# A hybrid decoder layer on one core: state layout, order of the value projections and of the SSM outputs in the mixing stage

## The chip, the core and the metric

The kernel runs on one core of a Trainium2 chip. The metric is the device time of one execution in microseconds. Three runs of the kernel before took 994.3, 994.25 and 993.5 us; the median is 994.25 us.

The engines are named as in the profile: PE (TensorE, matrix products, with PEld for its weight loads), DVE (VectorE), ACT (ScalarE), POOL (GpSimd) and SP (SyncE, whose queue issues nearly all DMAs here). Each engine works through its own queue in order and waits for others on semaphores.

## What is computed

One decoder layer for 512 tokens of width 1024, in float32: a SwiGLU block, a mixing stage and a second SwiGLU block, each between two RMS norms. The change lies in the mixing stage:

```python
h = rms_norm(x, mix_pre_g[l])
proj = h @ w_mix_in[l]                       # (512, 1024) @ (1024, 2048)
q, k, v, u = jnp.split(proj, [512, 1024, 1536], axis=-1)
attn = dilated_attention(q, k, v)            # 8 heads of 64, ALiBi, three dilations
ssm = s5_mixer(u, ...)                       # 32 groups of 16 channels, 64 complex states
mixed = jnp.concatenate([attn, ssm], axis=-1) @ w_mix_out[l]
x = x + rms_norm(mixed, mix_post_g[l])
```

The S5 mixer runs the recurrence state(t) = a * state(t-1) + B u(t) over the 512 tokens, reads out y = Re(C state) + D u, and returns gelu(y) * sigmoid(gelu(y) @ w_glu + b_glu).

## The kernel before

Activations lie transposed: channels on the 128 partitions, 512 tokens along the free axis. Every large product is split into three, with weights and activations as a high and a low part (`mm3`, L123: high x high, high x low, low x high). A weight tile arrives by one DMA as `wraw` (3 buffers), ACT casts the high part `whi` (L91), and DVE, or POOL where `pool=True`, subtracts to get the low part `wlo` (L93).

**The mixing stage** (`mix`, L821) has these pieces of PE work, in an order that the program fixes by hand:

- Projections (`proj`): 16 chunks of 128 output channels, 24 matmuls each. A generator `pieces` hands them out in halves of 12 matmuls; `f()` runs one half. Chunks 0 to 3 are q, 4 to 7 k, 8 to 11 v (two heads each), 12 to 15 u. DVE takes each result from PSUM as qT, kT or vT (L842, L844).
- Scores (`attn_scores`, L759) of a head pair `hp`: PE writes q*k, DVE adds the bias and takes the row extremum `nm` (L782), ACT takes the exponential and its row sum `den` (L784), DVE the reciprocal `rd` (L786), and the rows are scaled: those of the first head on ACT (L790), those of the second on DVE (L792).
- `turn` (L796) transposes the scaled scores on PE and copies them on ACT (L808); `turn_v` (L870) does it for v (copy `vn` on ACT, L876); `values` multiplies them into `pv`, which ACT and DVE split into the high and low parts of `cat`.
- The SSM: chunks of T = 4 tokens, 128 chunks in 8 super-chunks of 16. `states` (L881) computes each chunk's own contribution to the states `Hs`; `scan` (L1032), a generator whose steps are handed out by `go()`, or by `fg()` together with a projection half, runs on DVE alone: 15 steps inside all super-chunks at once, then 7 carry steps from super-chunk to super-chunk (`car`), then the carries multiplied back into all positions, 4 of 16 state blocks at a time. `outputs` (L888) computes four blocks of y from the shifted states and the weights `w2`, and the gelu.
- Output tiles (`out_attn`, `mo`, weights `wmoa`) for the attention half; `glu` with weights `wgl` for the gated SSM half (result `so`); the SSM half of the output product is done in `boundary` (L255, `yt`, weights `tw` loaded by `load_tail` from `wmot`), together with the norms and the first products of the next stage.

In `Hs` the chunk index is (super-chunk, position) with the position innermost, so that one scan step reads and writes every 16th element (64 bytes apart):

```python
h = Hs.rearrange("p q n (s i) -> p q n s i", i=SI)
step(h[:, :, :, :, i], h[:, :, :, :, i - 1], b1(pw[:, 0, :, 0]), b1(pw[:, 1, :, 0]), [NP, SC])
```

Instructions wrapped in `fix` keep the order of the program; the others are placed between them when the program is built. The order of the pieces of the stage is:

```python
sc = scores(1); f(); states(0); states(4); turn_v(0); states(8); states(12)
for hp in (2, 3):
    sc = scores(hp); fg(2); turn_v(hp - 1); fg(); values(hp - 1, pt)
```

## Time and profile before

| | |
|---|---|
| Median of three runs | 994.25 us |
| Profiled execution, its own time | 996.23 us |
| Span of its trace, first to last instruction | 994.4 us |
| Busy share of the span | PE 96%, DVE 55%, ACT 37%, POOL 23% |
| Mean granted TensorE clock | 0.981 of full speed |
| Chain that ended last | PE 84%, DVE 8%, issue 3%, ACT 3% |

A profile shows one execution. A row of its timeline gives start, duration, engine, line, operation and tile; in brackets the idle time before it and what ended the idle time. "Windows" are stretches of the span with each engine's busy time and the granted clock. The trace calls the tiles `w1` and `w2` both `w`. The mixing stage lies between about 404 and 589 us of the span, and the boundary to the second SwiGLU block behind it.

### The profile page before, as it was taken

Reading aid. Unit: us, or ns where it says so; the run is one execution under the profiler, and the core shown is the slowest. Engines: PE = TensorE matmul, PEld = TensorE weight load, DVE = VectorE, ACT = ScalarE, POOL = GpSimd, SP = SyncE. Lnnn points to the kernel's source line nnn. Section 1 sums busy time; section 2 is a strip of 40 time slices with the busy share of each in tenths; the row PEclk is TensorE's granted clock in tenths of the full one; section 3 lists DMA queues with packets and bytes.
Section 4 is the critical chain, followed back from the end, with each engine's and each line's share of the span. In section 5 each row is a group of like instructions: output and inputs, shape, how many; then the busy total and the mean of one; then the engine's idle time right before and its main releaser. Section 6 shows DMA issues by size and latency. Waiting matters only on the chain.

```text
span 994.4 us, 12883 instructions
## 1 busy us (share of the span) xinstructions
PE 958.3 (96%) x5088; PEld 800.3 (80%) x5088; DVE 544.7 (55%) x938; ACT 367.9 (37%) x604; POOL 231.8 (23%) x135
## 2 busy tenths in 40 slices
PE   9999999999999999999798789999999999999996
PEld 7888888888888899777566679888888888888885
DVE  7997124552356449467879656664215532554326
ACT  7353234521233225184443634444323222232312
POOL 2322122222233134200000423522013202321300
PEclk9999999999999999999899889999999999999998
DMA  7323334443333320661212620132332323233302
GB/s 256 105 86 111 116 102 148 131 148 103 106 127 106 106 86 22 191 191 59 64 33 96 202 64 23 52 97 85 106 107 85 102 92 103 85 106 126 107 1 85
DMA packets 38605, 102.48 MB, mean 103 GB/s; under 512 B 7664, under 2 KB 10736, under 8 KB 38000
## 3 DMA queue, kind: packets, MB, share of 16 engines
q1 hardware_dynamic: 37680, 98.50, 31.2%
q10 hardware_dynamic: 864, 3.15, 0.9%
q8 instruction: 40, 0.66, 0.3%
q14 instruction: 21, 0.17, 0.1%
HBM read 94.03 MB, written 7.60 MB: 102 GB/s over the span
## 4 chain that ended last, share of the span: by engine, by line
PE 84%; DVE 8%; issue 3%; ACT 3%; DMA 1%; POOL 1%; SPq 0%; DVEq 0%; POOLq 0%; ACTq 0%
PE gu L119 45%; PE yo L119 20%; PE yt L119 6%; PE prj L119 4%; PE first L119 4%; ACT sc L784 1%; DVE Hs L1035 1%; DVE xl L142 1%; PE pv L119 1%; DVE wlo L93 1%; PE st L119 1%; DVE x L301 1%; DVE sx L1035 1%; PE pt L806 1%; PE gl L119 1%
## 5 line engine op out<-in xcount | busy, mean ns | idle before, releaser
L91 ACT CAST whi<-wraw 128x1024 fp32r<-128x1024 f32 (+5 forms) x161 | 155.9, 970 | 323.9 <-PE gu L119 128.1
L93 POOL TENSOR_TENSOR wlo<-wraw,whi 128x1024 fp32r<-128x1024 f32 (+2 forms) x63 | 159.0, 2523 | 480.2 <-ACT whi L91 480.2
L119 PE MATMUL gu<-xh,whi 128*128 128x512 f32 x656 | 257.5, 393 | 0.0
L119 PE MATMUL gu<-xh,wlo 128*128 128x512 f32 x656 | 255.4, 389 | 0.0
L119 PE MATMUL gu<-xl,whi 128*128 128x512 f32 x656 | 255.3, 389 | 0.0
L93 DVE TENSOR_TENSOR wlo<-wraw,whi 128x1024 fp32r<-128x1024 f32 (+5 forms) x98 | 112.8, 1154 | 114.4 <-ACT whi L91 114.0
L119 PEld LDWEIGHTS gu<-xh,wlo 128*128 128x128 f32 x656 | 123.1, 188 | 26.0
L119 PEld LDWEIGHTS gu<-xh,whi 128*128 128x128 f32 x656 | 123.2, 188 | 25.0 <-issue 0.4
L119 PEld LDWEIGHTS gu<-xl,whi 128*128 128x128 f32 x656 | 123.2, 188 | 24.9
L394 DVE TENSOR_TENSOR ut<-gu,rs 128x512 f32<-128x512 f32 x41 | 28.3, 689 | 103.7 <-PE gu L119 103.7
L139 DVE TENSOR_TENSOR al<-ut,ah 128x512 fp32r<-128x512 f32 x44 | 69.0, 1569 | 25.0 <-ACT ah L138 24.8
L93 POOL TENSOR_TENSOR tw<-wraw,tw 128x1024 fp32r<-128x1024 f32 x8 | 19.4, 2430 | 163.7 <-ACT tw L91 163.7
L392 DVE TENSOR_TENSOR gt<-gu,rs 128x512 f32<-128x512 f32 x41 | 28.2, 689 | 50.8 <-PE gu L119 50.8
L119 PE MATMUL yo<-ah,whi 128*128 128x512 f32 x144 | 56.0, 389 | 0.0
L119 PE MATMUL yo<-al,whi 128*128 128x512 f32 x144 | 56.0, 389 | 0.0
L119 PE MATMUL yo<-ah,wlo 128*128 128x512 f32 x144 | 56.0, 389 | 0.0
L119 PE MATMUL yo<-whi,ah 128*128 128x512 f32 x144 | 56.0, 389 | 0.0
L119 PE MATMUL yo<-wlo,ah 128*128 128x512 f32 x144 | 56.0, 389 | 0.0
L119 PE MATMUL yo<-whi,al 128*128 128x512 f32 x144 | 56.0, 389 | 0.0
L138 ACT CAST ah<-ut 128x512 fp32r<-128x512 f32 x44 | 27.2, 621 | 58.2 <-DVE ut L395 58.2
L119 PE MATMUL first<-xl,whi 128*128 128x256 f32 (+1 forms) x144 | 44.5, 309 | 2.5 <-DVE xl L142 2.3
L119 PE MATMUL first<-xh,whi 128*128 128x256 f32 (+1 forms) x144 | 44.5, 309 | 0.9 <-ACT xh L141 0.9
(188 smaller groups left out, 1478.6 us busy)
## 6 DMA issues: line engine op xcount, KB each, us to landing
wraw<-w2i SPq DMA_DIRECT2D x44, 512.0 KB, 3.5
wraw<-w1i SPq DMA_DIRECT2D x42, 512.0 KB, 3.5
wraw<-w2o SPq DMA_DIRECT2D x18, 512.0 KB, 3.4
wraw<-wmi SPq DMA_DIRECT2D x16, 512.0 KB, 3.6
wraw<-w1o SPq DMA_DIRECT2D x16, 448.0 KB, 3.3
x<-xT SPq DMA_DIRECT2D x8, 256.0 KB, 4.5
w1d<-w1s SPq DMA_DIRECT2D x8, 256.0 KB, 2.8
w2d<-zb SPq DMA_DIRECT2D x2, 1024.0 KB, 4.9
```

Source lines behind the costliest of these rows:

```text
L91: fix(self.nc.scalar.copy(out=hi, in_=raw))
L93: fix(eng.tensor_tensor(out=lo, in0=raw, in1=hi.bitcast(F32), op=ALU.subtract))
L119: i = self.nc.tensor.matmul(*a, **k)
L138: nc.scalar.copy(out=hi, in_=src)
L139: nc.vector.tensor_tensor(out=lo, in0=src, in1=hi.bitcast(F32), op=ALU.subtract)
L142: fix(nc.vector.scalar_tensor_tensor(out=lo, in0=src, scalar=scale, in1=hi.bitcast(F32), op0=ALU.mult, op1=ALU.subtract))
L301: fix(nc.vector.tensor_tensor(out=xk, in0=t, in1=xk, op=ALU.add))
L392: nc.vector.tensor_tensor(out=gt, in0=o[f][0], in1=r, op=ALU.mult)
L394: nc.vector.tensor_tensor(out=ut, in0=o[f][1], in1=r, op=ALU.mult)
L784: nc.scalar.activation(out=so, in_=so, func=AF.Exp, bias=nm[:, t:t + 1], scale=-1.0, accum_out=den[:, t:t + 1])
L806: self.fix(nc.tensor.transpose(b[i][:, o:o + P], sc[:, c:c + P], self.ident))
L1035: tt = lambda o, x, y, op: self.fix(self.nc.vector.tensor_tensor(out=o, in0=x, in1=y, op=op))
```

## The change

The parts are these.

1. `states` writes the states with the position outermost and the super-chunk innermost (`(i s)`, `(s i)` before), one position later than before, and the last position into a tile of its own, `ends`. One scan step then touches runs of 8 neighbouring elements. The carries are kept in position 0 of `Hs` itself, with zero for the first super-chunk, so `outputs` reads 128 columns instead of 127 shifted ones. There are 6 carry steps instead of 7; the last part handles 15 positions x 8 super-chunks (480 elements an operation) instead of 7 x 16 (448). The reordering of u (`uT`) writes the new order; `glu`'s result is put back into the order of tokens where `so` is written.
2. A head pair's v projection comes ahead of its predecessor's scores: `f()` ahead of `scores(1)`, `fg(5)` for `fg(4)`, `fg()` for `fg(2)` behind `scores`, `fg(3)` for `fg(2)` at the end.
3. For head pairs 0 and 1 both heads are scaled on DVE; for 2 and 3 both on ACT, and the reciprocal is a power of -1 on POOL.
4. `outputs(0)` to `outputs(3)` stand between the output tiles 3 to 6; `w2` takes `wraw` buffers (before: `whi`). `glu` runs its first two tiles over three of four input blocks, then the fourth; both `wgl` tiles are loaded ahead; `zg` is scaled on ACT ahead of `glu`. `go(...)` counts follow.
5. The low halves of `tw` and `wgl` are made on DVE (POOL before).
6. `boundary` starts with tiles 0 and 1 over three of four input blocks, then the fourth for both.

```diff
+        b2 = [self.bank("yt")[:, :HT] for _ in range(2)]
+        for ks in (range(NT - 1), (NT - 1,)):
+            for m in range(2):
+                for k in ks:
+                    th, tl = tail(k)
+                    self.mm3(b2[m], tw[0][:, m, k], tw[1][:, m, k], th[:, hs[0]], tl[:, hs[0]], k == 0, k == NT - 1)
...
-            nc.vector.reciprocal(out=rd, in_=den)
+            if hp < 2:
+                nc.vector.reciprocal(out=rd, in_=den)
+            else:
+                nc.gpsimd.tensor_tensor(out=rd, in0=den, in1=self.mone, op=ALU.pow)
...
-                if i == 0:
+                if hp < 2:
+                    nc.vector.tensor_scalar_mul(so, so, rd[:, t:t + 1])
+                else:
                     nc.scalar.activation(out=so, in_=so, func=AF.Copy, scale=rd[:, t:t + 1])
-                else:
-                    nc.vector.tensor_scalar_mul(so, so, rd[:, t:t + 1])
...
-            dj = lambda v: v.rearrange("p (c j) -> p j c", j=T)
-            nc.vector.tensor_tensor(out=ut.rearrange("p (j c) -> p j c", j=T), in0=dj(o0[m]), in1=dj(r), op=ALU.mult)
+            nc.vector.tensor_tensor(out=ut.rearrange("p (j i s) -> p s i j", j=T, s=SC),
+                                    in0=o0[m].rearrange("p (s i j) -> p s i j", j=T, s=SC),
+                                    in1=r.rearrange("p (s i j) -> p s i j", j=T, s=SC), op=ALU.mult)
...
-                nc.scalar.copy(out=Hs[:, c, n4:n4 + 4].rearrange("p n k -> p (n k)"), in_=b)
+                b = b.rearrange("p (n k) -> p n k", k=NCH)
+                nc.scalar.copy(out=Hs[:, c, n4:n4 + 4, SC:], in_=b[:, :, :NCH - SC])
+                nc.scalar.copy(out=ends[:, c, n4:n4 + 4], in_=b[:, :, NCH - SC:])
...
-            w2 = self.wp.tile([P, 2, 4, P], F32, name="w2", tag="whi", bufs=4)
+            w2 = self.wp.tile([P, 2, 4, P], F32, name="w2", tag="wraw", bufs=3)
...
-        sc = scores(1)
         f()
+        sc = scores(1)
...
-        fg(4)
+        fg(5)
         for hp in (2, 3):
             sc = scores(hp)
-            fg(2)
+            fg()
...
-        tail = lambda c: self.load_tail(a["wmot"], c, True)
+        tail = lambda c: self.load_tail(a["wmot"], c, False)
...
         for n4 in range(4):
             outputs(n4)
+            if n4 < 3:
+                if n4 == 0:
+                    go()
+                out_attn(4 + n4)
+                tail(n4)
...
+        for m in range(2):
+            glu(m, range(3))
+        for m in range(2):
+            glu(m, (3,))
+        glu(2)
         tail(3)
+        glu(3)
         out_attn(7)
...
-        h = Hs.rearrange("p q n (s i) -> p q n s i", i=SI)
+        h = Hs.rearrange("p q n (i s) -> p q n i s", s=SC)
...
-            step(h[:, :, :, :, i], h[:, :, :, :, i - 1], b1(pw[:, 0, :, 0]), b1(pw[:, 1, :, 0]), [NP, SC])
+            step(ends if i == SI - 1 else h[:, :, :, i + 1], h[:, :, :, i], b1(pw[:, 0, :, 0]), b1(pw[:, 1, :, 0]),
+                 [NP, SC])
```

How this moves instructions is seen at three places. The first is DVE's queue at the scores of head pair 2 (`ISA sc,nm` is the bias and extremum, `vT` the value projection of head pair 1, `sx` and `Hs` the scan). Before, the end of that group of scores:

```order
L782 ISA sc,nm<-sc,bias 128x256
L782 ISA nm 128x1
L786 RECIPROCAL rd<-den 128x4 x2
L792 TENSOR_SCALAR sc<-sc,rd 128x128
L792 TENSOR_SCALAR sc<-sc,rd 128x256
L792 TENSOR_SCALAR sc<-sc,rd 128x384
L792 TENSOR_SCALAR sc<-sc,rd 128x512
L844 TENSOR_TENSOR vT<-prj,rs 128x512
```

Now, the beginning of that group:

```order
L1064 TENSOR_TENSOR Hs<-Hs,sx 128x16x8 x2
L858 TENSOR_TENSOR vT<-prj,rs 128x512
L1064 TENSOR_TENSOR sx<-pw,Hs 128x256 x2
L1064 TENSOR_TENSOR Hs<-Hs,sx 128x32x8
L793 ISA sc,nm<-sc,bias 128x512
L793 ISA nm 128x1
```

vT stood behind the reciprocals and four scalings, and stands now ahead of the first row of scores; reciprocals and scalings have left the queue here.

The second is ACT's queue at the same place (`den` is written by the exponentials, `vn` is the transposed v). Before:

```order
L790 ACTIVATE sc<-sc,rd 128x384
L790 ACTIVATE sc<-sc,rd 128x512
L784 ACTIVATE sc,den<-sc,nm 128x384
L784 ACTIVATE sc,den<-sc,nm 128x256
L91 CAST whi<-wraw 128x1024
L876 COPY vn<-vt 128x512
```

Now:

```order
L806 ACTIVATE sc<-sc,rd 128x384
L806 ACTIVATE sc<-sc,rd 128x512
L795 ACTIVATE sc,den<-sc,nm 128x384
L795 ACTIVATE sc,den<-sc,nm 128x256
L892 COPY vn<-vt 128x512
L806 ACTIVATE sc<-sc,rd 128x128
```

`vn` keeps its place behind all eight exponentials and four scalings; four more scalings follow it.

The third is SP's queue of DMAs at the SSM outputs (`w<-w2d` is the tile `w2` of one `outputs`). Before:

```order
L97 DMA wraw<-wmoa 128x512 x3
L891 DMA w_4696<-w2d 128x2x512
L891 DMA w_4754<-w2d 128x2x512
L97 DMA wraw<-wmot 128x1024
L891 DMA w_4812<-w2d 128x2x512
L97 DMA wraw<-wmoa 128x512
L891 DMA w_4870<-w2d 128x2x512
```

Now:

```order
L910 DMA w_4654<-w2d 128x2x512
L99 DMA wraw<-wmoa 128x512
L99 DMA wraw<-wmot 128x1024
L910 DMA w_4737<-w2d 128x2x512
L99 DMA wraw<-wmoa 128x512
L99 DMA wraw<-wmot 128x1024
L910 DMA w_4820<-w2d 128x2x512
L99 DMA wraw<-wmoa 128x512
L99 DMA wraw<-wmot 128x1024
L910 DMA w_4903<-w2d 128x2x512
```

Each `w2` now stands between the weights of two output tiles and shares their three buffers. By the waits of the built program the third `w2` is loaded into the buffer of the second and waits for PE's last read of it, the end of `outputs(1)`; the fourth waits for the low half of output tile 6; the `wgl` tile behind it for `outputs(2)`, and the last `wmot` for `outputs(3)`.

More of the change, by code (lines that the diff above doesn't have):

```diff
@@ L58, in __init__ @@
         nc.scalar.activation(out=self.mhalf, in_=self.ones[:, :1].to_broadcast([P, 4]), func=AF.Copy, scale=-0.5)
+        self.mone = self.cst.tile([P, 4], F32, name="mone")
+        nc.vector.memset(self.mone, -1.0)
         self.sm = self.cst.tile([P, 52], F32, name="sm")
@@ L310, in boundary @@
         V, G, fx = nc.vector, nc.gpsimd, self.fix
-        for m in range(KD):
+        b2 = [self.bank("yt")[:, :HT] for _ in range(2)]
[5 more added lines that the diff above has]
+        for m in range(2):
+            gather(0, m, 1, b2[m].unsqueeze(1))
+        squares(0, 0, 2, V)
+        for m in range(2, KD):
             b = product(0, m)
@@ L879, in mix @@
         Hs = self.b16("Hs").rearrange("p (q n) (b k) -> p q (n b) k", q=2, k=NCH)
+        ends = ap.tile([P, 2, NP, SC], F32, name="ends", tag="ends", bufs=1)
         def states(n4):
@@ L951, in mix @@
         cat = self.b16("cat", F32R)
-        scan = self.scan(ap, Hs)
+        scan = self.scan(ap, Hs, ends)
         def go(n=1):
@@ L1006, in mix @@
         st = self.b16("so", F32R)
         so = [st[:, :4], st[:, 4:]]
-        def glu(m2):
-            wh, wl = self.load(a["wgl"][m2], (8, P), pool=m2 == 0)
-            for mm in range(2):
-                m = 2 * m2 + mm
-                o = self.bank("gl")
-                for k in range(4):
-                    self.mm3(o, wh[:, 4 * mm + k], wl[:, 4 * mm + k], zt[:, k], zt[:, 4 + k], k == 0, k == 3)
+        wg = [[v[:, 4 * m:4 * m + 4] for v in w] for w in (self.load(a["wgl"][m2], (8, P)) for m2 in range(2))
+              for m in range(2)]
@@ L1016, in glu @@
+        og = {}
+        def glu(m, ks=range(4)):
+            if m not in og:
+                og[m] = self.bank("gl")
+            for k in ks:
+                self.mm3(og[m], wg[m][0][:, k], wg[m][1][:, k], zt[:, k], zt[:, 4 + k], k == 0, k == 3)
+            if 3 in ks:
                 t = self.tmp("gt")
-                nc.scalar.activation(out=t, in_=o, func=AF.Tanh, scale=0.25, bias=self.gh[:, 48 + m:49 + m])
+                nc.scalar.activation(out=t, in_=og[m], func=AF.Tanh, scale=0.25, bias=self.gh[:, 48 + m:49 + m])
@@ L1018, in glu @@
                 t2 = self.tmp("go")
[L1019 to L1027 removed]
+                nc.vector.scalar_tensor_tensor(out=t2, in0=t, scalar=1.0, in1=zg[:, m], op0=ALU.add, op1=ALU.mult)
@@ L1028, in mix, with scan @@
+                v = lambda w: w.rearrange("p (s i j) -> p j i s", j=T, s=SC)
+                self.split(v(so[0][:, m]), v(so[1][:, m]), t2.rearrange("p (j i s) -> p j i s", j=T, s=SC))
+        for m in range(2):
+            glu(m, range(3))
+        for m in range(2):
+            glu(m, (3,))
+        glu(2)
         tail(3)
+        glu(3)
         out_attn(7)
         return y, lambda i: (so[0][:, i], so[1][:, i])
-    def scan(self, ap, Hs):
-        tt = lambda o, x, y, op: self.fix(self.nc.vector.tensor_tensor(out=o, in0=x, in1=y, op=op))
+    def scan(self, ap, Hs, ends):
+        V = self.nc.vector
+        tt = lambda o, x, y, op: self.fix(V.tensor_tensor(out=o, in0=x, in1=y, op=op))
@@ L1036, in scan @@
         MUL, ADD, SUB = ALU.mult, ALU.add, ALU.subtract
         nb = 4
-        h = Hs.rearrange("p q n (s i) -> p q n s i", i=SI)
+        h = Hs.rearrange("p q n (i s) -> p q n i s", s=SC)
         pw = self.pw
         def tmp(shape):
-            t = ap.tile([P, nb * (SC - 1) * SI], F32, name="sx", tag="scan", bufs=4)
+            t = ap.tile([P, nb * (SI - 1) * SC], F32, name="sx", tag="scan", bufs=3)
             n = math.prod(shape)
@@ L1059, in scan @@
         for i in range(1, SI):
-            step(h[:, :, :, :, i], h[:, :, :, :, i - 1], b1(pw[:, 0, :, 0]), b1(pw[:, 1, :, 0]), [NP, SC])
+            step(ends if i == SI - 1 else h[:, :, :, i + 1], h[:, :, :, i], b1(pw[:, 0, :, 0]), b1(pw[:, 1, :, 0]),
+                 [NP, SC])
             yield
-        c = ap.tile([P, 2, NP, SC], F32, name="car", tag="car", bufs=1)
-        self.fix(self.nc.vector.tensor_copy(out=c, in_=h[:, :, :, :, SI - 1]))
+        self.fix(V.memset(h[:, :, :, 0, :1], 0.0))
+        self.fix(V.tensor_copy(out=h[:, :, :, 0, 1:], in_=ends[:, :, :, :SC - 1]))
         yield
-        for s in range(1, SC):
-            step(c[:, :, :, s], c[:, :, :, s - 1], pw[:, 0, :, SI - 1], pw[:, 1, :, SI - 1], [NP])
+        for s in range(2, SC):
+            step(h[:, :, :, 0, s], h[:, :, :, 0, s - 1], pw[:, 0, :, SI - 1], pw[:, 1, :, SI - 1], [NP])
             yield
         for n in range(0, NP, nb):
-            bp = lambda v: v[:, n:n + nb].unsqueeze(2).to_broadcast([P, nb, SC - 1, SI])
-            bs = lambda q: c[:, q, n:n + nb, :SC - 1].unsqueeze(3).to_broadcast([P, nb, SC - 1, SI])
-            d = h[:, :, n:n + nb, 1:, :]
+            nn = slice(n, n + nb)
+            shape = [nb, SI - 1, SC]
+            c = h[:, :, nn, 0]
+            bp = lambda q: pw[:, q, nn, :SI - 1].unsqueeze(3).to_broadcast([P] + shape)
+            bc = lambda q: c[:, q].unsqueeze(2).to_broadcast([P] + shape)
+            d = h[:, :, nn, 1:]
             for q in range(2):
-                t1, t2 = tmp([nb, SC - 1, SI]), tmp([nb, SC - 1, SI])
-                tt(t1, bp(pw[:, 0]), bs(q), MUL)
-                tt(t2, bp(pw[:, 1]), bs(1 - q), MUL)
+                t1, t2 = tmp(shape), tmp(shape)
+                tt(t1, bp(0), bc(q), MUL)
+                tt(t2, bp(1), bc(1 - q), MUL)
                 tt(d[:, q], d[:, q], t1, ADD)
                 tt(d[:, q], d[:, q], t2, SUB if q == 0 else ADD)
-                yield
+            yield
     def run(self, parts="fmg"):
```

28 lines of the change are left out of this document (9 added, 19 removed).

## The prediction

> **What bounds the kernel now.** PE is busy 96% of the span, so only time in which PE waits, or runs at a lower clock, can be won. I read the windows of the trace over the mixing stage first (columns: stretch, length, then busy time of PE, PEld, DVE, ACT, POOL with counts, granted clock, DMA share, GB/s; the sum is over all eight stretches).
>
> ```profile
> 432.00:454.00 22.00, 20.85 (x147) 16.55 (x144) 13.16 (x32) 17.09 (x40) 0.00 (x0) 1.00 0.38 124
> ...
> 478.00:494.00 16.00, 10.24 (x46) 7.24 (x46) 11.87 (x28) 7.43 (x19) 0.00 (x0) 0.79 0.18 52
> 494.00:522.00 28.00, 25.79 (x132) 19.28 (x131) 21.79 (x64) 11.93 (x32) 0.00 (x0) 0.94 0.16 47
> 522.00:545.00 23.00, 20.06 (x98) 14.93 (x96) 22.59 (x63) 6.64 (x14) 0.00 (x0) 1.00 0.29 96
> ...
> 560.00:584.00 24.00, 19.27 (x68) 14.19 (x67) 15.75 (x16) 12.86 (x20) 5.83 (x3) 0.79 0.38 122
> 584.00:606.00 22.00, 18.04 (x138) 17.64 (x137) 9.49 (x13) 6.13 (x11) 5.00 (x3) 0.92 0.15 49
> sum 174.00, PE 151.94 PEld 121.13 DVE 126.25 ACT 78.39 POOL 19.50; mean PE 18.99 PEld 15.14 DVE 15.78 ACT 9.80 POOL 2.44
> ```
>
> PE is idle 174.00 - 151.94 = 22.1 us. Length less busy time gives it by stretch: 1.15, 5.8, 2.2, 2.9, 4.7 and 4.0, and 1.3 are left for the two not shown. Four stretches also ran at a lower clock; busy time by (1 - clock) prices that at 2.2, 1.5, 4.0 and 1.4, together 9.1 us. So **31 us** can be won here. The waits of PE by releaser (total, times, longest) name the causes:
>
> ```profile
> PE vt L874 <- DVE vT L844: 8.5, 3, 5.8
> PE gl L119 <- ACT zz L138: 3.0, 2, 2.4
> PE yt L119 <- ACT so L141: 2.2, 1, 2.2
> PE mo L119 <- DVE wlo L93: 1.8, 1, 1.8
> ...
> PE gl L119 <- DVE zz L139: 1.7, 2, 1.2
> PE ys L119 <- issue: 1.3, 2, 0.9
> ```
>
> From which idle time on the clock falls is read from PE's timeline:
>
> ```profile
> 470.00 2.43 PE L119 MATMUL sc<-kT,qT 64*128 64x512 f32 x16
> ...
> 477.73 0.39 PE L119 MATMUL prj<-xh,wlo 128*128 128x512 f32 x1
> 483.87 1.11 PE L874 MATMUL vt<-ident,vT 128*128 128x128 f32 x4 [5.75 <-DVE vT L844]
> ...
> 513.16 0.66 PE L874 MATMUL vt<-ident,vT 128*128 128x128 f32 x4 [2.21 <-DVE vT L844]
> ...
> 514.41 0.63 PE L119 MATMUL prj<-xh,wlo 128*128 128x512 f32 x1
> ...
> 543.14 0.50 PE L119 MATMUL mo<-cat,wlo 128*128 128x512 f32 x1 [1.76 <-DVE wlo L93]
> ...
> 543.94 0.40 PE L119 MATMUL mo<-cat,wlo 128*128 128x512 f32 x1
> ```
>
> After 2.21 us of idle time a matmul took 0.63 us instead of 0.39; after 1.76 us it took 0.40. I take some 2 us idle as the edge, and 2 us as the price behind it (between the 1.5 and 2.2 above). At full clock the 24 matmuls between the first two rows start 0.23 us apart.
>
> **The change, part by part.** The sum is made against the profiled execution's own 996.23 us, which lies 1.98 us above the median of the runs.
>
> *1. Scan.* DVE's timeline at the first scan step, then groups of DVE by form (count, busy us, mean ns):
>
> ```profile
> 455.32 1.13 DVE L1035 TENSOR_TENSOR sx<-pw,Hs 128x256 f32<-128x256 f32 x2
> 456.37 1.34 DVE L1035 TENSOR_TENSOR Hs<-Hs,sx 128x256 f32<-128x256 f32 x3
> ...
> L93 DVE TENSOR_TENSOR wlo<-wraw,whi 128x1024 fp32r<-128x1024 f32 x15 | 18.3, 1222 | 9.6 <-ACT whi L91 9.6
> L1035 DVE TENSOR_TENSOR sx<-pw,Hs 128x256 f32<-128x256 f32 x30 | 16.7, 597 | 0.2
> L1035 DVE TENSOR_TENSOR Hs<-Hs,sx 128x128 f32<-128x128 f32 x30 | 10.2, 390 | 0.2
> ...
> L860 DVE TENSOR_TENSOR uT<-first,rs 128x512 f32<-128x512 f32 x4 | 4.0, 1052 | 0.0
> ...
> L293 DVE TENSOR_TENSOR acc<-acc,sq 128x256 f32<-128x256 f32 x2 | 0.8, 422 | 0.2 <-ACT sq L290 0.2
> ```
>
> A step takes 2.4 us (455.32 to 457.71). 256 elements cost 597 ns at a distance of 64 bytes and 422 ns in one run; the change's runs of 8 are not in the trace. Their price lies between these ends, and I take the contiguous one, since a run of 8 is nearer to it: 3 x 0.18 for the 256s and 2 x 0.1 for the 128s make the step 0.75 us shorter, 11 us of DVE in 15 steps and none of PE by itself. A projection takes PE 24 x 0.23 = 5.5 us; two steps, an eviction (0.7) and a low half (1.2) take DVE 6.7 us before and 5.2 now. So DVE no longer falls behind there.
>
> *2. v ahead of scores.* DVE's timeline, then ACT's, at the scores of pair 2:
>
> ```profile
> 474.20 0.68 DVE L782 CUSTOM_DVE_ANT_0 sc<-sc,bias 128x512 f32<-128x512 f32 x1
> ...
> 483.13 0.68 DVE L844 TENSOR_TENSOR vT<-prj,rs 128x512 f32<-128x512 f32 x1
> ...
> 478.70 1.90 ACT L790 ACTIVATE sc<-sc,rd 128x128 f32<-128x128 f32 x4
> ...
> 481.60 1.03 ACT L91 CAST whi<-wraw 128x1024 fp32r<-128x1024 f32 x1
> 485.02 0.59 ACT L876 COPY vn<-vt 128x512 f32<-128x512 f32 x1 [2.39 <-PE vt L874]
> ```
>
> At pair 1 the waits of the first stretch go: vT no longer stands behind the scores, and the four scalings of 1.9 us leave ACT. **-1.15.** At pairs 2 and 3 vT precedes the scores, so `vt` finds it ready. What is late next is `vn`, which stays behind the exponentials on ACT, and `values` waits for it. From the first row of scores ACT needs 481.60 - 474.20 = 7.4 us until it is free for `vn`, 0.6 for the copy, and some 0.6 more because the reciprocal now comes from POOL. Ahead of that row stand vT (0.9 with its signal) and three scan operations (1.0). So `vn` is there 10.5 us after PE begins the scores. PE's own work up to `values` is 2.4 (scores) + 2.75 + 0.5 + 2.75 (two half projections and `vt`) = 8.4 us. It waits 2.1 us, and more where the reciprocal is late:
>
> ```profile
> 410.34 1.66 POOL L182 TENSOR_TENSOR r<-nv,mhalf 128x2 f32<-128x2 f32 x1 [6.33 <-DVE nv L180]
> ...
> L182 POOL TENSOR_TENSOR p<-nv,mhalf x4: 706/706/719, 369.5 to 622.5; 128x2 f32<-128x2 f32 x4
> ```
>
> The power takes POOL 0.71 us as a rule and took 1.66 once, so the wait lies between 2.1 and 3.1 us. I take 2.5, and 2 of clock. Pair 2: 8.0 before, 4.5 now, **-3.5**. Pair 3: 3.7 before, 4.5 now, **+0.8**. Behind `vn` on ACT stand four scalings (1.9), which `turn` needs only after `values`.
>
> [...]
>
> *3. SSM outputs.* `outputs(0)` needs only the first 8 of the 32 operations of the last scan part, while PE still has `pv` and 30 output matmuls to do. The wait for `wlo` (1.8) goes; what else is idle in that stretch (1.1), a wait for `cat`, I leave at 0.8. The issue waits (1.3) give place to waits for `w2`: the third is loaded only behind `outputs(1)`, the fourth behind the low half of tile 6. DMA issues, median us to landing in the last column, and the loads of `um`:
>
> ```profile
> w<-w2d SPq DMA_DIRECT2D x4, 512.0 KB, 4.6
> ...
> wraw<-w2i SPq DMA_DIRECT2D x7, 512.0 KB, 3.5
> ...
> DMA to landing us min/median/max: 5.4/7.0/8.0
> ```
>
> It lands 3.5 to 4.6 us later, and the output tile between covers 12 x 0.23 = 2.75: 0.8 to 1.9 us each, 1.4 taken. Before 4.2, now 0.8 + 2.8, **-0.6**.
>
> *4. POOL's low halves and `glu`.* Beside a low half on POOL, DVE is slowed:
>
> ```profile
> 576.68 2.39 POOL L93 TENSOR_TENSOR wlo<-wraw,whi 128x1024 fp32r<-128x1024 f32 x1 [11.35 <-ACT whi L91]
> ...
> 577.22 2.79 DVE L1020 SCALAR_TENSOR_TENSOR go<-gt,zg 128x512 f32<-128x512 f32 x1 [2.83 <-ACT gt L1017]
> ...
> 581.32 1.21 DVE L1020 SCALAR_TENSOR_TENSOR go<-gt,zg 128x512 f32<-128x512 f32 x1
> ```
>
> 2.79 for 1.21 us. DVE gets five low halves of 1.2 us, which fit beside its 15.75 of 24 us. `glu` now has 18 matmuls (4.1 us) that need only the first three SSM blocks. But the last `tw` stands ahead of the last `zz` on ACT and DVE, and its DMA starts only when `outputs(3)` has ended: 4.0 + 1.0 (cast) + 1.2 + 0.7 (`zz`) = 6.9 us, of which 2.8 are not covered. Clock: 1.5, between nothing and 4. Before 8.7, now 4.3, **-4.4**.
>
> *5. Start of the boundary.* The last `so` comes some 3.9 us behind the end of `glu`: tanh, `go`, cast and low half at 0.6 to 0.7 each, and a weight cast and its low half between. Output tile 7 (2.75) and 18 matmuls of 256 columns (some 2.2) stand in front. The waits for `so` and the clock behind them go, **-5.4**.
>
> *At nothing:* `uT` writing elements 512 bytes apart (0.7 to 1.3 us each; the row before has 1.05 for a strided read) ends near 419, and `states` uses it near 443. The copies of `ends` (8, under 0.4 each) and the scaling of `zg` (4, 0.6 each) lie on ACT, busy 17 of 22 and 13 of 24 us. The strided write of `so` is covered by the 4.9 us. Where such a cover is gone, each costs its own time once.
>
> Sum: -1.15 - 3.5 + 0.8 - 0.6 - 4.4 - 5.4 = **-14.25**: 982.0 by the profiled execution, **980.0** by the median.
>
> **Rivals.** *The clock holds.* The waits of 2.5 us are near the edge. The three clock terms (5.5) fall away: 974.5. Against it speaks the row at 513.16. [...]
>
> *Runs of 8 are no faster than single elements*, so the change doesn't do what it says for the scan. Steps stay at 2.4 us, DVE falls 1.2 us behind a projection over 2.5 projections less what it idled, and both waits for `vn` grow by 2.8: +5.6, and 0.7 at the last step: 986.3. For it: the form is not in the trace. Against it: only the nearness of a run of 8 to a long run.
>
> *The weight ring decides (slower).* `w2`, the output weights and the last `tw` wait for one another in three buffers. If a landing takes the 8.0 us of the last row (several loads in flight) instead of 4.05, three waits grow by 3.95, and each passes 2 us idle, which adds 4.5 of clock: 16.4 against the gain of 14.25, or 996.4. It decides from a landing of about 7.3 us, where 3 x 3.25 + 4.5 reach 14.25. Against it: two `w2` loads issued together still had 4.6.
>
> **How the numbers follow.** Forecast 0.57; clock holds 0.18; scan no faster 0.17; weight ring 0.08, of which 0.05 ends slower and 0.03 within 0.2%, about what a measurement of this kernel can tell from no change. So faster 0.92, same 0.03, slower 0.05. The range runs from the clock rival with waits at their lower ends, 974, to the scan rival with the longest landings, 988.5; the ring and the tails are left out.
>
> **What would show it.** `sx` of 256 elements near 0.42 us; `vt` without a wait; a wait of `pv` for ACT's `vn` near 2.5 us, twice, with matmuls of 0.63 behind; `ys` waiting 1 to 2 us for a DMA at its third and fourth block; `yt` starting without a wait; no DVE operation of 2.4 us beside POOL. Wrong would be a scan step still above 2.2 us, or waits of `ys` above 3 us.

## The result, and the profile after

| | before | changed |
|---|---|---|
| Median of the runs | 994.27 us (4) | 980.78 us (4; 978.9 to 983.03) |
| Ratio of the two, 95% interval | | 0.9865 (0.9839 to 0.9891) |
| The same kernel again, second series | 995.07 us (11) | 982.31 us, ratio 0.9875 (0.9855 to 0.9894) |
| Profiled execution, its own time | 996.23 us | 978.9 us |
| Span of its trace | 994.4 us | 977.1 us |
| Mean granted TensorE clock | 0.981 | 0.995 |

The kernel became 1.3% faster; 980.0 us was forecast. In the second series one of six executions of the changed kernel took 1183.45 us at a granted clock of 0.752; it is left out of the ratio, and the median of the other five is 982.11 us. The sum is right, but several of its terms are not, and their errors cancel. The two traces show this, piece by piece. The table takes one matmul at each seam of the mixing stage and compares its start in the two traces; the last column is what the piece that ends there gained or lost.

| PE begins | before | changed | moved | piece | forecast |
|---|---|---|---|---|---|
| first projection | 406.75 | 405.38 | -1.37 | -1.37 | none, untouched code |
| `pt` behind `values` of pair 0 | 453.98 | 450.95 | -3.03 | **-1.66** | -1.15 |
| `pt` behind `values` of pair 1 | 492.29 | 482.60 | -9.69 | **-6.66** | -3.5 |
| `pt` behind `values` of pair 2 | 520.38 | 508.91 | -11.47 | **-1.78** | +0.8 |
| `mo` behind `values` of pair 3 | 529.63 | 518.17 | -11.46 | 0.0 | none |
| `glu` | 560.78 | 554.39 | -6.39 | **+5.07** | -0.6 |
| output tile 7 | 581.02 | 567.69 | -13.33 | **-6.94** | -4.4 |
| first sums of squares of the boundary (`st`) | 605.34 | 588.93 | -16.41 | **-3.08** | -5.4 |
| end of the span | 994.4 | 977.1 | -17.3 | -0.9 | none, untouched code |

The six bold pieces sum to -15.05 us. The first and the last row are not the change's work: in the profiled execution of before, the code there ran twice at half clock, and in that of the changed kernel it did not. Windows of the trace of before at these two places (columns as in the prediction: stretch, length, busy time of PE, PEld, DVE, ACT, POOL, granted clock, DMA share, GB/s):

```profile
401.15:404.56 3.41, 3.41 (x18) 3.41 (x17) 0.00 (x0) 0.98 (x2) 2.78 (x3) 0.50 0.47 195
636.64:640.05 3.41, 3.41 (x18) 3.41 (x18) 1.71 (x1) 1.68 (x2) 1.77 (x3) 0.50 0.02 5
```

PE is busy throughout at a clock of 0.50 (in the first its matmuls of 256 columns start 0.21 us apart, behind it 0.12), so each stretch costs up to half its length. That is in part why the two profiled executions lie 17.3 us apart and the medians only 13.5. Up to their last microseconds the trace of before has nine such windows of 3.41 us at half clock, that of the changed kernel one. PE's waits from 404 to 610 us fell from 22.0 to 14.4 us, so more than half of the 17.3 us between these two executions is clock.

The waits of PE in the changed kernel from 404 to 610 us (total, times, longest), to be held against the list in the prediction:

```profile
PE ys L121 <- DMA w<-w2d: 5.6, 2, 3.1
PE pv L121 <- ACT vn L892: 4.1, 2, 2.1
PE yt L121 <- DVE so L141: 1.4, 2, 0.7
PE mo L121 <- DVE cat L141: 1.4, 1, 1.4
PE gl L121 <- ACT zz L140: 0.9, 1, 0.9
PE gl L121 <- DVE zz L141: 0.8, 1, 0.8
PE yt L121 <- ACT so L140: 0.2, 1, 0.2
```

All waits of `vt` for vT are gone (8.5 us before). Two new ones stand in their place: `values` (`pv`) waits for the copy `vn` on ACT, and the SSM outputs (`ys`) wait for the DMA of `w2`. PE's timeline at both places:

```profile
480.29 2.37 PE L121 MATMUL pv<-ptt,vn 128*64 128x512 f32 x16 [2.00 <-ACT vn L892]
...
538.35 0.42 PE L121 MATMUL ys<-um 128*32 128x128 f32 x8
541.85 0.64 PE L121 MATMUL ys<-Hs,w 128*32 128x128 f32 x16 [3.07 <-DMA w<-w2d]
...
550.33 1.08 PE L121 MATMUL ys<-Hs,w 128*32 128x128 f32 x16 [2.57 <-DMA w<-w2d]
```

Behind the wait of 3.07 us sixteen matmuls took 0.64 us, behind the shorter one of 2.57 us they took 1.08. So the length of a wait alone does not decide whether clock is lost; this became the first question of the runs.

DVE's groups by form in the changed kernel (count, then busy us and mean ns) answer the scan's term:

```profile
L1064 DVE TENSOR_TENSOR sx<-pw,Hs 128x256 f32<-128x256 f32 x30 | 11.3, 419 | 0.2
...
L1064 DVE TENSOR_TENSOR Hs<-Hs,sx 128x128 f32<-128x128 f32 x28 | 6.9, 287 | 0.3
...
L141 DVE TENSOR_TENSOR so<-go,so 128x512 fp32r<-128x512 f32 x4 | 5.5, 1406 | 3.0 <-ACT so L140 2.9
```

In runs of 8 neighbours 256 elements took 419 ns, as long as in one long run before (422), against 597 in single elements; 128 took 287 against 390. The last row belongs to the boundary, and comes up again below.

### The profile page after: what moved, and what is told of

Its sections match the earlier page's. It is cut to its first block, busy times and chain, and to the rows that moved or that the text cites. A ratio compares the mean times of both kernels' runs of the same rounds, so it can differ in the third digit from the quotient of the medians.

```text
span 977.1 us, 12902 instructions
## 1 busy us (share of the span) xinstructions
PE 948.4 (97%) x5088; PEld 792.6 (81%) x5088; DVE 532.9 (55%) x938; ACT 372.3 (38%) x616; POOL 223.5 (23%) x134
## 4 chain that ended last, share of the span: by engine, by line
PE 86%; DVE 7%; ACT 3%; DMA 2%; issue 1%; POOL 0%; DVEq 0%; POOLq 0%; ACTq 0%
PE gu L121 46%; PE yo L121 20%; PE prj L121 6%; PE yt L121 5%; PE first L121 4%; PE st L121 1%; DVE sx L1064 1%; DVE Hs L1064 1%; DVE xl L144 1%; DMA wraw<-wmot 1%; DVE x L303 1%; PE pt L820 1%; ACT sc L795 1%; DMA w<-w2d 1%; PE idle L121 1%
## 5 line engine op out<-in xcount | busy, mean ns | idle before, releaser
L95 POOL TENSOR_TENSOR wlo<-wraw,whi 128x1024 fp32r<-128x1024 f32 (+2 forms) x62 | 156.3, 2521 | 525.9 <-ACT whi L93 525.9
L406 DVE TENSOR_TENSOR ut<-ut,gt 128x512 f32<-128x512 f32 x44 | 40.7, 927 | 3.7
```

The costliest lines, as they stand in the source:

```text
L95: fix(eng.tensor_tensor(out=lo, in0=raw, in1=hi.bitcast(F32), op=ALU.subtract))
L406: nc.vector.tensor_tensor(out=ut, in0=ut, in1=gt, op=ALU.mult)
```

## The experiments

Each kernel is the changed kernel with one edit, except for the three combinations at the end. All were timed beside the kernel before, in three series; the median of before was 995.07 us in the first two and 992.74 in the third (the last four rows), so the ratio is what compares. Where the interval of a run overlaps those of the changed kernel (0.9839 to 0.9891 and 0.9855 to 0.9894), as with `w2early` and `b2_old`, and barely with `vorder23`, `scan_strided`, `pool_low`, `rd_vn` and `rd_w2`, the time alone does not settle the difference, and the waits in the trace have to carry it.

| run | median us | ratio to before | 95% interval |
|---|---|---|---|
| again | 982.31 | 0.9875 | 0.9855 to 0.9894 |
| w2early | 979.81 | 0.985 | 0.9829 to 0.987 |
| vnearly | 976.46 | 0.9816 | 0.9797 to 0.9835 |
| vorder23 | 978.36 | 0.9836 | 0.9816 to 0.9855 |
| scan_strided | 985.43 | 0.9907 | 0.9891 to 0.9923 |
| pool_low | 985.45 | 0.9902 | 0.9887 to 0.9917 |
| b2_old | 984.56 | 0.9896 | 0.9876 to 0.9915 |
| rd_dve | 974.23 | 0.9793 | 0.9779 to 0.9808 |
| rd_vn | 975.04 | 0.982 | 0.9794 to 0.9845 |
| rd_w2 | 974.63 | 0.9817 | 0.9792 to 0.9843 |
| all3 | 973.52 | 0.9799 | 0.9773 to 0.9825 |
| glu_old | 985.36 | 0.9917 | 0.9894 to 0.994 |

### again: what does a wait cost in clock?

No edit; a second profile of the changed kernel.

> The changed kernel unaltered, for a second profile. In the first one TensorE's half-clock stretches last multiples of 3.41 us, and the six of the kernel before begin on one grid of 3.413 us; a wait of 3.07 us that the grid cuts in two kept the clock, one of 2.57 us inside one of its windows lost it. Grid theory: the same waits come back within 0.3 us (values for ACT's vn 2.0 and 2.1, the SSM outputs for w2 3.1 and 2.6), but half clock stands behind other ones of them than before, and the time lies anywhere between 978 and 984 us. Rival, the length of a wait decides: again the clock is lost behind the wait of the fourth SSM output and behind no other, and the time is 979 us within 0.7.

The waits came back: 2.00 and 2.12 us for `vn`, 3.08 and 3.03 for `w2` (the last one 0.4 us above what was expected; the executions took 980.73 to 984.55 us). But now half clock stood behind both waits for `vn`, which had kept the clock the first time. Windows of 3.41 us, of the first profile and then of this one, around the same wait of 2.00 us:

```profile
478.38:481.79 3.41, 1.50 (x8) 0.63 (x10) 1.64 (x4) 2.73 (x9) 1.04 (x1) 1.00 0.23 73
481.79:485.20 3.41, 3.41 (x27) 2.78 (x24) 1.82 (x5) 3.28 (x7) 0.00 (x0) 1.00 0.02 5
```

```profile
480.55:483.96 3.41, 1.41 (x7) 0.49 (x7) 1.77 (x6) 2.73 (x8) 1.04 (x1) 1.00 0.24 77
483.96:487.37 3.41, 3.41 (x17) 1.81 (x14) 1.09 (x3) 2.70 (x6) 0.00 (x0) 0.50 0.00 0
507.87:511.28 3.41, 1.29 (x7) 0.76 (x7) 1.33 (x6) 3.16 (x9) 0.57 (x1) 1.00 0.20 65
511.28:514.70 3.42, 3.42 (x12) 1.22 (x11) 0.50 (x1) 2.42 (x5) 0.43 (x1) 0.50 0.00 0
```

In the second profile the wait lay wholly inside one window, in the first about 0.1 us of it fell into the window before. PE was busy for 1.41 and for 1.50 us of 3.41. The half-clock stretches of this profile begin at 402.06, 483.98, 511.28 and 555.66 us: 24, 32 and 45 times 3.413 us behind the first. Those of the kernel before, at 401.12, 483.04, 513.76, 564.96, 588.85 and 636.64, stand 24, 33, 48, 55 and 69 such steps behind the first. The stretches of every other trace here stand whole steps apart too. Against the first instruction the grid stands elsewhere in each execution: the one stretch of the first profile, at 550.09, begins 0.54 us past a whole number of steps, those of this one 2.70 and those of before 1.76. So the kernel starts somewhere in the grid: a single wait of 2 to 3 us cost either nothing more (2.00 and 3.07 in the first profile) or half of 3.41 us, about 1.7 (2.00 in this one), as chance has it. Six traces have the two waits of 2.0 and 2.1 us for `vn` unaltered (both profiles of the changed kernel, `w2early`, `pool_low`, `glu_old` and `b2_old`). Of these twelve waits the five that lay wholly inside one window lost the clock behind them, and the seven that the grid cut kept it. The wait of 3.08 us for `w2` was cut by the grid here too (1.2 and 1.9 us) and again kept the clock. The rival, that the length decides, is refuted. A window in which PE was busy for 1.41 us (41%; 480.55 to 483.96 above) was enough to lose the clock in the next one. Where the line runs stays open: in the first profile a window with the same 1.41 us of busy time (539.85 to 543.26), at the end of the wait of 3.07, kept the clock.

### vorder23: was it the order of v?

```diff
-        fg(5)
+        fg(4)
         for hp in (2, 3):
             sc = scores(hp)
-            fg()
+            fg(2)
             turn_v(hp - 1)
...
-                fg(3)
+                fg(2)
```

> For head pairs 2 and 3 the order of before (a half projection behind the scores, v behind them too); scan layout and scalings as changed. Theory, the waits for vT went because the scan got shorter and DVE lost the scalings, not because v was moved: no wait for vT over 0.5 us comes back, values still waits for vn some 2 to 3 us, since vn has gone behind the second head's scalings and a cast, and the time is within 1.5 us of the changed kernel, 979 to 982 us. Rival, the move of v did it: waits for vT of over 1.5 us are back in both pairs, and the time is 984 to 988 us.

PE's waits at head pairs 1 to 3, of this run:

```profile
PE pv L121 <- ACT vn L892: 3.3, 2, 2.1
```

No wait for vT came back, though v stands behind the scores again on PE and DVE. The time, 978.4 us, is even somewhat below the changed kernel's and below what was expected: three half projections instead of two lie between scores and `values`, and the second wait for `vn` is 1.15 us, not 2.12. For pairs 2 and 3 the move of v was therefore not what removed the 8 us of waits. What is left of the change at this place are the shorter scan steps, and the reciprocals and scalings that left DVE's queue ahead of vT. How they share it was not separated: the next run takes the scan back, but with v ahead of the scores, and no run puts the scalings back.

### scan_strided: the layout alone

```diff
+        nc.gpsimd.memset(Hs[:, :, :, :SC], 0.0)
...
-        h = Hs.rearrange("p q n (i s) -> p q n i s", s=SC)
+        h = Hs.rearrange("p q n (s i) -> p q n i s", s=SC)
...
-            shape = [nb, SI - 1, SC]
+            shape = [nb, SC, SI - 1]
...
-            d = h[:, :, nn, 1:]
+            d = h[:, :, nn, 1:].rearrange("p q n i s -> p q n s i")
```

> The scan alone walks the states in the old order again (a step touches every 16th element); states, uT, so and everything else stay as changed, so the states are written in one order and scanned in another, and the output is not the layer's. The 30 sx of 256 should take about 0.60 us again in place of 0.42, and a step 2.4 us in place of 1.75. Theory, the layout is what lets DVE keep up: DVE falls behind the projections by 0.4 to 0.9 us each, vT is 1 to 2 us late ahead of the scores, vt waits for it and the states are ready later for the SSM outputs: 4 to 9 us slower than the changed kernel, 985 to 990 us. Rival, the order of DVE's queue is all that counts, and the 10 us are slack: within 1.5 us of the changed kernel, 980 to 983 us.

DVE's group by form, then PE's longest waits, of this run:

```profile
L1066 DVE TENSOR_TENSOR sx<-pw,Hs 128x256 f32<-128x256 f32 x30 | 16.6, 596 | 0.2
```

```profile
PE pv L121 <- ACT vn L892: 8.4, 2, 5.6
PE ys L121 <- DMA w<-w2d: 4.8, 2, 4.6
```

The states are written in one order and scanned in another here, so this kernel does not compute the layer. The duration is that of before, and the kernel is 3 to 5 us slower than the changed one. The place was not the one expected for the run, but the one that the prediction's rival on the scan had named: `vt` does not wait, since vT stands ahead of the scores, but the rows of scores behind it on DVE come late, with them ACT's exponentials, and with these `vn`: 5.63 us in pair 1 in place of 2.00, and 2.76 in place of 2.12 in pair 2. A late DVE shows as a wait for ACT here.

### vnearly and rd_dve: two ways to shorten the wait for vn

The first puts `vt` behind the scores on PE and so `vn` among the exponentials on ACT (`behind` is called in `attn_scores` after its matmuls); the second puts the reciprocals of pairs 2 and 3 back on DVE.

```diff
+        if behind:
+            behind()
...
-            sc = scores(hp)
-            fg()
-            turn_v(hp - 1)
-            fg()
+            sc = scores(hp, lambda: turn_v(hp - 1))
+            fg(2)
```

> The transposes of v stand right behind the scores, and its copy vn behind four of the eight exponentials, not behind all and four scalings. Theory, the waits of values for vn (2.0 and 2.1 us) are only ACT's order: they go, at most 0.7 us comes back where turn waits for the second head's scalings in pair 3: 3.4 us faster than the changed kernel, 977 us. Rival, ACT is the limit of that stretch: turn waits as long as values did, and the time stays at 981 us.

```diff
-            if hp < 2:
-                nc.vector.reciprocal(out=rd, in_=den)
-            else:
-                nc.gpsimd.tensor_tensor(out=rd, in0=den, in1=self.mone, op=ALU.pow)
+            nc.vector.reciprocal(out=rd, in_=den)
```

> The reciprocals of pairs 2 and 3 on DVE again (0.17 us) and not as a power on POOL (1.09 us). Theory, the power stands on the chain to vn: it ends 0.9 us earlier, and both waits of values for vn fall from 2.0 and 2.1 to 1.1 and 1.2 us, below what costs clock: 2 to 4 us faster than the changed kernel, 977 to 979 us. Rival, DVE's queue now stands still behind den: the waits for vn fall, but vT, the low halves or the scan come later by as much, and the time stays at 981 us.

In the changed kernel the power on POOL takes 1.09 us, and ACT's scalings, which stand ahead of `vn`, wait for it (POOL's group by form; ACT's waits from 470 to 510 us):

```profile
L800 POOL TENSOR_TENSOR rd<-den,mone 128x4 f32<-128x4 f32 x4 | 4.4, 1094 | 92.2 <-ACT sc L795 92.2
```

```profile
ACT sc L806 <- POOL rd L800: 3.2, 4, 1.0
```

PE's waits with vn early, then with the reciprocal on DVE:

```profile
PE ys L121 <- DMA w<-w2d: 2.8, 2, 1.9
PE mo L121 <- DVE cat L141: 2.6, 1, 2.6
```

```profile
PE ys L121 <- DMA w<-w2d: 2.8, 2, 2.5
PE pv L121 <- ACT vn L889: 2.1, 2, 1.0
PE yt L121 <- DVE so L141: 1.4, 2, 0.7
PE gl L121 <- DVE zz L141: 0.8, 1, 0.8
PE mo L121 <- DVE cat L141: 0.7, 1, 0.7
```

With vn early the waits for `vn` are gone, and part of the gain returns as a longer wait for `cat`, whose low half stands in DVE's queue among the last scan operations (2.57 us in place of 1.44). With the reciprocal on DVE the waits fall from 2.00 and 2.12 to 1.02 and 1.03 us, as expected, but the gain was larger than expected: 974.2 us, 6 to 8 us below the changed kernel. Against the first profile of the changed kernel (each has one half-clock stretch inside the stage) the spans differ by 5.8 us; the sum of PE's waits from 404 to 610 us falls from 14.4 to 8.8. Of these 5.6 us, 2.1 are `vn`, 0.7 `cat`, 0.5 the third `w2` and 2.3 the fourth. At the fourth, PE arrives 1.45 us later after the issue than in the first profile, since the third SSM output runs at half clock this time (the block takes 4.27 us in place of 2.61), and the tile lands 0.85 us sooner: most of the clock lost ahead of this DMA was time that PE would have waited. Why `cat` and the third `w2` come earlier was not followed further. So the waits that hang on the reciprocal itself are 2.1 us; clock behind them comes on top in some executions. The four of this run have granted clocks of 0.993 to 0.995, the first four of the changed kernel 0.989 to 0.995. Of the parts that were undone by themselves, the move of the reciprocal to POOL is the one that clearly makes the kernel slower. The order of the SSM outputs, whose piece became 5.1 us longer, and the moved scalings were not undone by themselves.

### w2early: the weights of the SSM outputs

```diff
-            w2 = self.wp.tile([P, 2, 4, P], F32, name="w2", tag="wraw", bufs=3)
-            nc.sync.dma_start(out=w2, in_=self.w2d[:, :, 4 * n4:4 * n4 + 4])
+            for i in {0: (0,), 1: (1, 2), 2: (3,), 3: ()}[n4]:
+                tag, bufs = ("wraw", 3) if i < 2 else ("whi", 4)
+                w2t[i] = self.wp.tile([P, 2, 4, P], F32, name="w2", tag=tag, bufs=bufs)
+                nc.sync.dma_start(out=w2t[i], in_=self.w2d[:, :, 4 * i:4 * i + 4])
+            w2 = w2t[n4]
```

> The third and fourth w2 are loaded one block earlier, into the ring of whi, and not behind wmot. Theory, the weight ring as such is the limit: the waits of the SSM outputs for w2 (5.6 us) go, but output tile 6, whose weights now wait for the end of the second SSM output, comes 1 to 2 us late, and glu's first weights, which wait for a low half of wmot, 2 to 4 us: together 1 to 3 us faster than the changed kernel, 978 to 980 us. Rival, only the place of w2 in SP's queue counts: no wait takes the place of the 5.6 us, and with the clock it gives 973 to 975 us.

In the changed kernel the third `w2` is issued at 535.78 us, right behind the end of the second SSM output, and 0.42 us behind a weight tile of the boundary of the same size (SP's queue: issue, its length):

```profile
535.36 0.33 SPq L99 DMA_DIRECT2D wraw<-wmot  x1
535.78 0.53 SPq L910 DMA_DIRECT2D w<-w2d  x1
```

PE goes on at 541.85, 6.07 us after the issue; the fourth is issued at 544.07, 1.51 us behind a tile of the boundary and 0.62 ahead of two for `glu`, and PE goes on at 550.33, 6.26 after it. The other traces hold the same loads with other neighbours. With a boundary tile 0.42 us ahead, the third landed in 5.5 to 6.1 us in eight traces, and once in 7.6; with the tile 0.93 us ahead in 5.1 (`vnearly`). With no weight tile issued in the 16 us ahead, the second landed in 4.1 to 4.6. With the boundary tile 1.51 us ahead, the fourth landed in 6.1 to 6.6 us where the tiles for `glu` followed 0.62 us behind, and in 5.1 to 5.8 where they followed some 1.8 us behind (`scan_strided`, `rd_dve`, `rd_vn`). Moved one block earlier, both are there in time, and PE waits for this instead:

```profile
PE mo L121 <- ACT whi L93: 1.8, 1, 1.8
PE yt L121 <- DVE so L141: 1.8, 1, 1.8
```

So 5.6 us of waits leave 1.8 at output tile 6 and somewhat more at the boundary, and the kernel gains 1 to 2.5 us against its two medians; the intervals overlap. As expected, output tile 6, whose weights wait for a buffer, takes over a part of the delay; the 2 to 4 us that were expected at `glu`'s first weights did not come.

### pool_low, glu_old, b2_old: the rest of the stage undone

```diff
-        tail = lambda c: self.load_tail(a["wmot"], c, False)
+        tail = lambda c: self.load_tail(a["wmot"], c, True)
...
-        wg = [[v[:, 4 * m:4 * m + 4] for v in w] for w in (self.load(a["wgl"][m2], (8, P)) for m2 in range(2))
+        wg = [[v[:, 4 * m:4 * m + 4] for v in w] for w in (self.load(a["wgl"][m2], (8, P), pool=True) for m2 in range(2))
```

> The low halves of wmot and wgl on POOL again, nothing else. Theory, a low half on POOL takes twice as long (2.4 us) and slows DVE beside it: the weight ring turns slower, w2 and glu's weights come 1 to 3 us late each, and DVE operations of over 2 us are back: 3 to 6 us slower than the changed kernel, 984 to 988 us. Rival, PE waits there for w2's landing and not for low halves: within 1.5 us of the changed kernel, 980 to 983 us.

```diff
-        for m in range(2):
-            glu(m, range(3))
-        for m in range(2):
-            glu(m, (3,))
+        for m in range(2):
+            glu(m)
```

> The changed kernel with glu's first tile done over all four blocks before the second. Theory, nine matmuls of cover (2.1 us) ahead of the fourth block are gone: waits for zz of 0.9 and 0.8 us become 3.8 us together, with 0 to 1.7 us of clock: 983 to 985 us. Rival, the fourth block is waited for by what follows in any order: within 1 us of the changed kernel, 981 to 982 us.

```diff
-        for ks in (range(NT - 1), (NT - 1,)):
+        for ks in (range(NT),):
```

> The boundary finishes tile 0 over all four blocks of so before tile 1. Theory, the new start covers only its own nine matmuls of 256 columns: PE waits 1.1 us more for so, with 1.7 us more where the grid of the clock falls badly: 982 to 984 us. Rival, it is the whole gain of 5.4 us that the prediction put there: 985 to 987 us.

With the low halves on POOL, DVE's low half of the last `zz` lies beside one of them (DVE's timeline, then POOL's):

```profile
564.14 2.42 DVE L141 TENSOR_TENSOR zz<-zg,zz 128x512 fp32r<-128x512 f32 x1 [1.04 <-ACT zz L140]
```

```profile
563.66 2.35 POOL L95 TENSOR_TENSOR tw<-wraw,tw 128x1024 fp32r<-128x1024 f32 x1 [0.68 <-ACT tw L93]
```

It takes 2.42 us, where it takes 0.69 in the changed kernel, and it ends 0.55 us behind the one on POOL, not much less than its own length. `glu` waits 1.95 us for it in place of 0.85, and the boundary 1.61 at once for `so`. The kernel is 3 to 5 us slower, as expected, though the waits for `w2` (6.4 us in place of 5.6 and 6.1) grew less than the 1 to 3 us each that were expected. `glu` in the old order waits 2.80 and 0.85 us in place of 0.87 and 0.85 and is 4 to 5 us slower by the ratio, somewhat more than the 1 to 4 that were expected; the old start of the boundary waits 2.55 us for `so` in place of 1.64. That is 0.9 us, where 1.1 was expected; its median, half a microsecond above the expected range, lies 2 to 4 us above the changed kernel's, of which 0.9 is seen as waits, and a half-clock stretch stood behind them at 576 us. So of the 5.4 us that the prediction put at the boundary, the new start itself accounts for these 0.9 us of waits and, as the grid falls, for clock behind them.

### rd_vn, rd_w2, all3: do the gains add?

These combine the edits above.

> The reciprocals of pairs 2 and 3 on DVE, and vn early. Theory, the two act on the same waits of values for vn, so the gains do not add: the 2.1 us of these waits that were left with the reciprocals on DVE go, and one half of that comes back as a longer wait for cat behind the scan, as in the run with vn early alone (2.6 us): 972 to 974 us. Rival, they add (5 and 7 us): 969 us.

> The reciprocals of pairs 2 and 3 on DVE, and the third and fourth w2 one block earlier. Theory, the ring limits the SSM stretch whatever the SSM outputs wait for: the waits for w2 (2.8 us) go, 1.5 to 2.5 us come back at output tile 6 and at the boundary for so, as with w2 early alone: 972 to 975 us. Rival, the waits for w2 are pure: 971 us.

> The three edits together. Theory: 970 to 973 us, below every single one; left are waits for cat, output tile 6, zz and so of 6 to 8 us together. Rival, DVE's scan is the limit now that PE comes earlier: the waits for cat and for the states grow by what was won, 973 to 975 us.

They do not add. All three lie between 973.5 and 975.0 us, beside a slightly faster kernel before, and none is apart from the reciprocal on DVE alone: the intervals of their ratios overlap. In the run with all three edits `pv`, `ys` and `mo` wait for neither `vn` nor `w2`, and PE waits elsewhere:

```profile
PE gl L121 <- ACT zz L140: 2.9, 1, 2.9
PE mo L121 <- DVE cat L141: 2.2, 1, 2.2
PE yt L121 <- DVE so L141: 1.9, 1, 1.9
```

8.2 us of waits are left in the stretch. `zz`, `cat` and `so` are all made by DVE and ACT out of what PE has just finished; coming earlier, PE waits for them longer. The expectation for the first of the three, 972 to 974 us, was missed by 1 us; the second lies within its 972 to 975. For the last, 973.5 us lies in the range of the rival (973 to 975) and 0.5 us above that of the theory. But of the two waits that grew most, for `zz` and for `cat`, only that for `cat` stands behind DVE's scan, and it stays open whether the scan is the new limit.

## Why the prediction came out, step by step

**What bounds the kernel.** Right: the gain is PE's idle time and its clock. The clock was read wrongly. "I take some 2 us idle as the edge" took two rows of one execution for a threshold. The runs show a grid of 3.41 us, on which the same wait of 2.00 us cost 0 (first profile) or about 1.7 us (second). The price of the clock was read from the mean clock of long stretches, which dilutes it: pair 2's 2.2 us were 3.0, half of the 2.6 and 3.4 us for which PE was busy in the two half-clock windows from 483.04 us on.

**1. Scan.** Right: 419 ns for 256 elements (420 forecast), 287 for 128. That the layout makes no PE time "by itself" but keeps DVE from falling behind fits the scan walked in the old stride, 3 to 5 us slower: the waits for `vn` grew by 3.6 and 0.6 us, where the rival had 2.8 twice. The rival "Runs of 8 are no faster than single elements" falls.

**2. v ahead of scores.** The new wait was right in place and nearly in size: 2.00 and 2.12 us for `vn`, 2.5 forecast. Mis-sized was its clock term of 2 us each: none in the first profile, about 1.7 twice in the second, and five times in the twelve waits seen. So pair 2 gave -6.7 in place of -3.5 (a wait of 2.00 for one of 5.75 with 3.0 of clock behind it) and pair 3 -1.8 in place of +0.8, which is what the rival "The clock holds" says; other executions lie between it and the forecast. Wrong was the cause that the heading names: for pairs 2 and 3 the order of v is worth nothing, and the old order is, if anything, faster (0.9836 against 0.9865 and 0.9875). The power on POOL took 1.09 us, inside the bounds of 0.71 and 1.66, where the reciprocal on DVE takes 0.17. Its price was put at 0.6 us, and undoing it gained 6 to 8, more than the 2.1 us of waits that are traced to it.

**3. SSM outputs.** The waits for the third and fourth `w2` came where they were forecast. Mis-sized was the landing: 4.05 us were taken, 6.0 and 6.2 measured, so that PE waited 3.07 and 2.57 us and not 1.4 each; a wait for `cat` of 1.44 (0.8 forecast) and one half-clock stretch (1.6) came on top. The piece cost 5.1 us where -0.6 was forecast, the largest single error; these terms make 5.1 of the 5.7 us between the two, and the rest was not followed. The row of 4.6 us that was quoted against long landings as "two `w2` loads issued together" is the median of four loads; the two that the trace merges into one row were issued 2.7 us apart and landed in 4.1 and 4.8 us. Here another tile of 512 KB started 0.42 us ahead of the third, and two more 0.62 us behind the fourth. The rival "the weight ring decides" had the right mechanism; its three waits were two, below the 7.3 us at which it would have decided.

**4. POOL's low halves and glu.** Right in mechanism: undoing either part costs 3 to 5 us in the whole. The last `tw` stood ahead of the last `zz`, as forecast (ACT's timeline in the changed kernel):

```profile
558.01 1.05 ACT L93 CAST tw<-wraw 128x1024 fp32r<-128x1024 f32 x1 [1.42 <-DMA wraw<-wmot]
558.97 0.61 ACT L140 CAST zz<-zg 128x512 fp32r<-128x512 f32 x1
```

Both halves of `zz` were ready 6.5 us behind `outputs(3)`, where 6.9 was forecast. Too careful was what is left of it: "of which 2.8 are not covered" became 0.87 + 0.85 us, without loss of clock, so -6.9 in place of -4.4. Not all low halves left POOL: those of the next stage's weights are still made there, and one of them slows a `so` on DVE (below).

**5. Start of the boundary.** Half right: the waits for `so` fell from 3.95 to 1.64 us, where "The waits for `so` and the clock behind them go" was forecast: -3.1 in place of -5.4. The mis-sized step is "The last `so` comes some 3.9 us behind the end of `glu`": it came 7.4 us behind it (567.8 to 575.2 us), more than the 4.9 us of PE work in front. ACT, DVE and POOL at this place in the changed kernel:

```profile
570.11 1.13 ACT L140 CAST so<-go 128x512 fp32r<-128x512 f32 x1 [2.64 <-DVE go L1044]
571.03 0.67 ACT L1042 ACTIVATE gt<-gl,gh 128x512 f32<-128x512 f32 x1
...
566.09 3.39 DVE L141 TENSOR_TENSOR so<-go,so 128x512 fp32r<-128x512 f32 x2 [1.74 <-ACT so L140]
569.39 0.68 DVE L1044 SCALAR_TENSOR_TENSOR go<-gt,zg 128x512 f32<-128x512 f32 x1
574.15 1.07 DVE L141 TENSOR_TENSOR so<-go,so 128x512 fp32r<-128x512 f32 x1
...
565.11 2.41 POOL L95 TENSOR_TENSOR wlo<-wraw,whi 128x1024 fp32r<-128x1024 f32 x1 [57.87 <-ACT whi L93]
```

ACT's queue stands at the third `so` until the third `go` comes from DVE, and DVE gets to this `go` only behind two `so`, the first of which takes 2.39 us beside the subtraction on POOL. So the tanh `gt` of the last tile begins 3.2 us behind the end of `glu`, and its chain up to the last `so` takes 4.2 us from there. That chain was near its size, although `so` is now written back into the order of tokens, which costs both engines more (ACT's and DVE's instructions on `so` in the changed kernel; minimum, median and maximum in ns):

```profile
L140 ACT CAST so<-go x4: 1126/1138/1164, 564.9 to 573.0; 128x512 fp32r<-128x512 f32 x4
L141 DVE TENSOR_TENSOR so<-go,so x4: 1071/1081/2391, 566.1 to 574.1; 128x512 fp32r<-128x512 f32 x4
```

Before, they took 632 and 694 ns, and the same two operations on `zz`, which is not reordered, take 0.61 and 0.68 us here. The 0.9 us that this adds to the last `so` were put under "At nothing", with the cover of the 4.9 us; with 3.9 us that cover would have reached, and what it missed are the 3.2 us ahead of the tanh. Some 0.7 us of the miss of 2.3 are not found in the waits.

**The signs.** As named were `sx` of 256 elements, `vt` without a wait and two waits of `pv` for `vn`, with matmuls at half clock behind them in the second profile only. Not as named: `ys` waited 3.07 and 2.57 us, where 1 to 2 was named and "waits of `ys` above 3 us" were to be a sign of being wrong; `yt` did not start without a wait; and a DVE operation of 2.39 us beside POOL is left. The ends of the range do not follow from the words either: the clock rival with the lower ends of its waits (2.1 and 0.8 us) gives 972.5 us and not 974, and the scan rival reaches 988.5 only if the waits for `vn` are taken at 3.1 us besides the longest landings.

**The sum.** The errors of -0.5, -3.2 and -2.6 at pairs 1 to 3 and of -2.5 in `glu` meet +5.7 in the SSM outputs and +2.3 at the boundary. The total of -14.25 beside the measured -15.05 is in part luck.

## What to carry to other kernels

When a wait moves from one engine to another, follow the whole chain behind it to its last instruction on the new engine: one microsecond more for a reciprocal, on an engine that was idle, lengthened two waits by 1 us each, since scalings and a copy stood behind it, and the kernel without it was 6 to 8 us faster. Price a DMA by what is issued right ahead of it and behind it on the same queue, not by the median of its kind: `w2`, 512 KB each time, landed in 4.1 to 7.6 us here. And read waits of 2 to 3 us as a lottery (of the twelve of 2.0 and 2.1 us five lost the clock behind them): shortening them can save the lost clock too, which one profile alone does not show. Behind the four waits for `vn` of 1.0 us in `rd_dve` and `rd_w2` none was lost.
